# The expert layer of an encoder trunk: TensorE's wide products, transpositions of the middle columns and sums, kept in the order of the program

## The chip, the cores and the metric

The kernel runs on one core of one Trainium2 chip. The metric is the device time of one execution in microseconds (us); less is better. TensorE is called PE here (its weight loads PEld), VectorE DVE, ScalarE ACT, GpSimd POOL and SyncE SP. Each engine works off its own queue in order, and engines wait for each other by semaphores.

## The reference

It is a two-layer encoder over 272 tokens of 1024 columns: attention and a dense SwiGLU, then a two-way RWKV-7 scan and a mixture of experts, each with a layer norm behind it. The change touches the experts alone:

```python
logits = x @ w_router + b_router                    # 256 tokens that count, 8 experts
gates  = top-2 of softmax(logits), renormalized
for e in range(8):                                  # 1024 -> 3584 -> 1024
    y += gates[:, e:e+1] * ((silu(x @ w_gate[e]) * (x @ w_up[e])) @ w_down[e])
out = layer_norm(ALPHA * h + y)
```

All is float32. Each expert has 44 MB of weights, all of which are read once.

## The kernel before

**Passes.** By the tokens that chose them, five experts are made wide (W, up to 128 tokens) and three narrow (N, up to 64); they are worked off in the order W N W W N W W N. Each expert is worked off in two halves of 1792 middle columns, so the loop `for n in range(16)` in `moe` (lines 1585 to 1637) has 16 passes, 0 to 15; passes 2, 3, 8, 9, 14 and 15 are narrow. A pass computes gate and up products for its half (x is the stationary operand, the weights stream), and between and behind them the down products of the half of the pass before (`down`, `down_wide`, `down_narrow`).

**Wide products.** A product in float32 is made of three faster ones. Each piece of 768 to 1024 columns of weights (called a part here) is cast on ACT to `w_hi` (line 124), and the rest `w_lo` = raw - `w_hi` is made on DVE or, for three parts of twelve, on POOL (line 127). There are four buffers of `w_hi` and four of `w_lo`. `stream_wide` (line 1404) then issues, for each of 16 parts of gate or up, four products on `w_hi` and two on `w_lo` (line 1414). `down_wide` issues through `mm3` (lines 134 to 136) one on `w_hi`, one on `w_lo`, and one on `w_hi` with the rest of the activations. Narrow products take the raw weights in full float32 (lines 1429 and 1478); they need neither cast nor rest.

**Middle columns.** The activations `hid` are made by a Silu on ACT (lines 1616 and 1627) and a multiplication on DVE (lines 1621 and 1629), then transposed on PE (lines 1445 and 1459) through the one PSUM tile `pt` into `hth` (and `htl`), of which there is one buffer: `step` functions that are called in the stream of the next pass behind parts 2, 6, 10 and 14.

**Gathers and sums.** The tokens of the next expert are gathered by products with a one-hot matrix (lines 1359, 1366, 1385, 1393), also through `pt`. The finished expert is copied from PSUM (line 1498 or 139) and summed into the tokens by products (line 1512) and a multiply-add on DVE (line 1514).

**The order.** The text of the program doesn't set the order inside an engine's queue. A planner takes each instruction as soon as it believes, by its own estimates of all durations and of the landing of loads, that its operands and buffers are there; among several the earlier in the text goes first. `keep_in_program_order` binds an instruction behind the one traced just before it on the same engine. That is an order of issue only: it adds no semaphore and no wait for that one's end. Before the change it binds the narrow products (lines 1429 and 1478) and a few others. Weights are loaded by SP (line 1556) into a ring of 17 buffers of 0.9 MB, in the order of the program.

Of the kernel before, what the change touches and what calls it, by code (L numbers as in the profile page):

```python
# [26 lines left out]
FT = 1792  # L27
NB = FT // 128
# [66 lines left out]
class Trunk:  # L95
# [15 lines left out]
    def load(self, src, r0, kt, c0, nc_, pitch):  # L111

        raw = next(self.raws)()[:, :kt * nc_].rearrange("p (k c) -> p k c", k=kt)
        self.nc.sync.dma_start(raw, self.row_ap(src, r0 * pitch + c0, [[pitch, 128], [128 * pitch, kt], [1, nc_]]))
        return raw
# [13 lines left out]
            self.parted_pool = self.parted  # L129
        return hi, lo  # L130

    def mm3(self, ps, wh, wl, xh, xl, start, stop):
        mm = self.nc.tensor.matmul
        mm(ps, wh, xh, start=start, stop=False)  # L134
        mm(ps, wh, xl, start=False, stop=False)  # L135
        return mm(ps, wl, xh, start=False, stop=stop)  # L136

    def split(self, hi, lo, src, eng=None):
        return self.nc.scalar.copy(hi, src), (eng or self.nc.vector).tensor_tensor(lo, src, hi.bitcast(F32), op=OP.subtract)
# [1264 lines left out]
    def stream_wide(self, psum, xe, load, steps):  # L1404

        ps = [psum.tile([128, 2, 512], F32, name="pgu", bufs=2) for _ in range(2)]
        mm = self.nc.tensor.matmul
        for k in range(NF):
            raw = load(k)
            for a in range(2):  # L1410
                wh, wl = self.part_of(raw[:, 896 * a:896 * a + 896])
                for i, (x, w) in enumerate(((0, wh), (1, wh), (0, wl))):
                    for b in range(2):
                        mm(ps[a][:, b, :448], xe[:, x, k, :], w[:, 448 * b:448 * b + 448], start=k == 0 and i == 0,  # L1414
                           stop=k == NF - 1 and i == 2)
                for f in steps.pop(2 * k + a, ()):
                    f()
        return ps
# [16 lines left out]
    def hidden_wide(self, mp, psum, s, H):  # L1435

        nc = self.nc

        def step(i0):
            if i0 == 0:  # L1440
                H['h'] = [mp.tile([128, NB, 128], F32R, name=n, bufs=1) for n in ("hth", "htl")]
            n = min(4, NB - i0)
            pt = psum.tile([128, 4, 128], F32, name="pt", bufs=1)
            for j in range(n):
                nc.tensor.transpose(pt[:, j, :], s[:, i0 + j:FT:NB], self.ident)  # L1445
            hh, hl = H['h']
            self.split(hh[:, i0:i0 + n, :], hl[:, i0:i0 + n, :], pt[:, :n, :])

        return [lambda i=i: step(i) for i in range(0, NB, 4)]

    def hidden_narrow(self, mp, psum, s, H):
        nc = self.nc

        def step(i0):
            if i0 == 0:
                H['h'] = mp.tile([128, NB, 64], F32, name="hth", bufs=1)
            pt = psum.tile([128, 7, 64], F32, name="pt", bufs=1)
            for j in range(7):
                nc.tensor.transpose(pt[:, j, :], s[64:128, i0 + j:FT:NB], self.ident[64:128, 64:128])  # L1459
            nc.vector.tensor_copy(H['h'][:, i0:i0 + 7, :], pt)  # L1460

        return [lambda i=i: step(i) for i in (0, 7)]

    def down_wide(self, h, load, pd, half, first, last):
        hh, hl = h
        for j in range(4 * half, 4 * half + 4):
            raw, cut = load(j), (0, 1024, FT) if j % 2 == 0 else (0, 768, FT)
            for a, b in zip(cut, cut[1:]):
                wh, wl = self.part_of(raw[:, a:b])
                for o, n, i, q, c in self.pieces(j, a, b):  # L1470
                    self.mm3(pd[q][:, c:c + n], hh[:, i, :], hl[:, i, :], wh[:, o - a:o - a + n], wl[:, o - a:o - a + n],
                             first and i == 0, last and i == NB - 1)

    def down_narrow(self, h, load, pd, half, first, last):
        for j in range(4 * half, 4 * half + 4):
# [15 lines left out]
    def combine(self, mp, psum, n, G, pd, last=False):  # L1491

        nc, Y = self.nc, {}

        def parts(q):
            if len(pd) == 1:
                Y[0] = Y[1] = [mp.tile([128, 512], F32, name="xs", bufs=1)]
                nc.scalar.copy(Y[0][0], pd[0][0])
                return
            y = mp.tile([128, 2, NF, 128], F32R, name=G['tag'], bufs=1).rearrange("p i f t -> p i (f t)")  # L1500
            Y[q] = [y[:, i, 512 * q:512 * q + 512] for i in range(2)]
            self.split(*Y[q], pd[q][0])

        def add(q, t):
            if last:

                ps = psum.tile([128, 512], F32, name=f"pd{q}", bufs=1) if t == 0 else wide()[:, q, :]
            else:
                ps = psum.tile([128, 512], F32, name=pd[q % len(pd)][1], bufs=1)
            os = G['os'][q][:, t, :]  # L1510
            for i, x in enumerate(Y[q]):
                nc.tensor.matmul(ps, os, x, start=i == 0, stop=i == len(Y[q]) - 1)  # L1512
            y = self.ymoe[:, t, 512 * q:512 * q + 512]
            nc.vector.scalar_tensor_tensor(y, ps, self.gate[:, t, n:n + 1], y, op0=OP.mult, op1=OP.add)

        def wide():
            if 'w' not in Y:
                Y['w'] = psum.tile([128, 2, 512], F32, name="pgu", bufs=2)
            return Y['w']

        if last:
            return [lambda: parts(0)] + [lambda q=q, t=t: add(q, t) for t in range(2) for q in range(2)]
        if len(pd) == 1:
            return [lambda: parts(0)] + [lambda q=q, t=t: add(q, t) for q in range(2) for t in range(2)]
        return [f for q in range(2) for f in (lambda q=q: parts(q), lambda q=q: add(q, 0), lambda q=q: add(q, 1))]

    def moe(self, ep, psums, scanp):
# [221 lines left out]
```

## Time and profile before

| | us |
|---|---|
| median of 3 runs | 1858.39 (1857.37 to 1863.82) |
| the profiled execution | 1862.5 |
| its span, first to last instruction | 1860.4 |
| PE busy in the span | 1699.6 (91%) |
| DVE busy | 1276.6 (69%) |
| ACT busy | 913.0 (49%) |
| POOL busy | 631.1 (34%) |

The expert layer takes from about 890 us of the span to about 1845 us. A row of a timeline gives the start (us from the span's start), the length, the engine, the line, output<-inputs and a count, and in brackets how long the engine was idle before it and what ended that. Rows that run on overlap a little, since matmuls are pipelined: the pace is read from start to start. In the windows, PEclk is the share of PE's full clock (2.4 GHz) that was granted.

### The profile page before, as it was taken

Reading aid. Unit: us, or ns where it says so; the run is one execution under the profiler, and the core shown is the slowest. Engines: PE = TensorE matmul, PEld = TensorE weight load, DVE = VectorE, ACT = ScalarE, POOL = GpSimd, SP = SyncE. Lnnn points to the kernel's source line nnn. Section 1 sums busy time; section 2 is a strip of 40 time slices with the busy share of each in tenths; the row PEclk is TensorE's granted clock in tenths of the full one; section 3 lists DMA queues with packets and bytes.
Section 4 is the critical chain, followed back from the end, with each engine's and each line's share of the span. In section 5 each row is a group of like instructions: output and inputs, shape, how many; then the busy total and the mean of one; then the engine's idle time right before and its main releaser. Section 6 shows DMA issues by size and latency. Waiting matters only on the chain.

```text
span 1860.4 us, 30513 instructions
## 1 busy us (share of the span) xinstructions
PE 1699.6 (91%) x11422; PEld 1359.5 (73%) x11422; DVE 1276.6 (69%) x2135; ACT 913.0 (49%) x1612; POOL 631.1 (34%) x551
## 2 busy tenths in 40 slices
PE   6999899987988988897999999999999999999996
PEld 5888899975666766676986567888856668888552
DVE  5786655578868896854896446989934469899332
ACT  4575444446334435433674235766723357677210
POOL 4322300148464554512353112444502125445101
PEclk9999899988978878897999999999999999999998
DMA  6322455541101000355769899998999999899992
GB/s 203 120 91 69 136 182 177 186 125 47 57 24 53 24 25 2 131 204 215 241 238 348 347 426 426 425 342 305 341 358 352 423 422 345 327 328 345 389 395 92
DMA packets 130737, 431.79 MB, mean 232 GB/s; under 512 B 13689, under 2 KB 78674, under 8 KB 130578
## 3 DMA queue, kind: packets, MB, share of 16 engines
q1 hardware_dynamic: 127202, 427.78, 61.6%
q10 hardware_dynamic: 3376, 1.95, 0.4%
q8 instruction: 92, 1.51, 0.3%
q14 instruction: 67, 0.55, 0.1%
HBM read 428.66 MB, written 1.05 MB: 231 GB/s over the span
## 4 chain that ended last, share of the span: by engine, by line
PE 38%; issue 5%; DVE 4%; POOL 1%; DMA 1%; ACT 1%; SPq 0%; DVEq 0%; POOLq 0%; ACTq 0%
PE pgu L1414 16%; PE pgu L1429 5%; PE pdn L1478 4%; PE pd L135 3%; PE pd L136 3%; PE pd L134 3%; DVE w_lo L127 2%; POOL w_lo L127 1%; DMA w_raw<-in_moe_w_down_dram 1%; PE pd L1512 1%; DVE hid L1621 1%; PE pt L1445 1%; PE pt L1359 1%; PE pt L1459 1%; ACT w_hi L124 0%
## 5 line engine op out<-in xcount | busy, mean ns | idle before, releaser
L127 DVE TENSOR_TENSOR w_lo<-w_raw,w_hi 128x896 fp32r<-128x896 f32 (+2 forms) x445 | 647.2, 1494 | 151.5 <-ACT w_hi L124 144.5
L124 ACT CAST w_hi<-w_raw 128x896 fp32r<-128x896 f32 (+2 forms) x580 | 537.2, 960 | 279.5 <-PE pd L136 70.6
L127 POOL TENSOR_TENSOR w_lo<-w_raw,w_hi 128x1024 fp32r<-128x1024 f32 (+1 forms) x135 | 335.3, 2484 | 629.6 <-ACT w_hi L124 445.3
L1414 PE MATMUL pgu<-w_hi,xe 128*128 128x448 f32 x1280 | 299.5, 369 | 2.4 <-DVE hid L1621 1.6
L1414 PEld LDWEIGHTS pgu<-w_hi,xe 128*128 128x128 f32 x1280 | 237.5, 188 | 26.8 <-issue 6.5
L1414 PE MATMUL pgu<-w_lo,xe 128*128 128x448 f32 x640 | 164.6, 369 | 4.7 <-DVE w_lo L127 4.6
L1429 PE MATMUL pgu<-w_raw,xs 128*64 128x448 f32 x768 | 158.1, 544 | 0.0
L1414 PEld LDWEIGHTS pgu<-w_lo,xe 128*128 128x128 f32 x640 | 118.5, 188 | 18.9 <-DVE w_lo L127 8.1
L135 PE MATMUL pd<-w_lo,hth 128*128 128x512 f32 (+1 forms) x320 | 121.3, 384 | 9.8 <-DVE w_lo L127 6.3
L136 PE MATMUL pd<-w_hi,htl 128*128 128x512 f32 (+1 forms) x320 | 119.8, 375 | 0.0
L1429 PEld LDWEIGHTS pgu<-w_raw,xs 128*64 128x64 f32 x768 | 59.1, 136 | 81.1 <-issue 76.9
L134 PE MATMUL pd<-w_hi,hth 128*128 128x512 f32 (+1 forms) x320 | 101.0, 375 | 4.1 <-ACT w_hi L124 4.1
L135 PEld LDWEIGHTS pd<-w_lo,hth 128*128 128x128 f32 x320 | 62.1, 194 | 28.7 <-DVE w_lo L127 8.3
L1478 PE MATMUL pdn<-w_raw,hth 128*64 128x512 f32 (+1 forms) x384 | 79.6, 542 | 0.0
L134 PEld LDWEIGHTS pd<-w_hi,hth 128*128 128x128 f32 x320 | 58.9, 194 | 17.3 <-ACT w_hi L124 5.7
L134 PE MATMUL pj<-xh,w_hi 128*128 128x272 f32 x192 | 60.1, 313 | 11.8 <-ACT w_hi L124 5.4
L136 PEld LDWEIGHTS pd<-w_hi,htl 128*128 128x128 f32 x320 | 62.2, 194 | 10.3 <-issue 0.7
L1478 PEld LDWEIGHTS pdn<-w_raw,hth 128*64 128x64 f32 x384 | 32.5, 137 | 37.8 <-issue 30.4
L136 PE MATMUL pj<-xh,w_lo 128*128 128x272 f32 x192 | 58.3, 304 | 0.6 <-DVE w_lo L127 0.6
L135 PE MATMUL pj<-xl,w_hi 128*128 128x272 f32 x192 | 58.0, 302 | 0.0
L1629 DVE TENSOR_TENSOR hid<-hid,pgu 64x896 f32<-64x896 f32 x12 | 13.0, 1091 | 62.3 <-ACT hid L1627 62.3
L153 POOL COPY ln_s<-ln_y 128x272 f32<-128x272 f32 x2 | 0.8, 414 | 156.2 <-DVE ln_y L150 156.2
(639 smaller groups left out, 3569.6 us busy)
## 6 DMA issues: line engine op xcount, KB each, us to landing
w_raw<-in_moe_w_down_dram SPq DMA_DIRECT2D x128, 896.0 KB, 7.5
w_raw<-in_moe_w_gate_dram SPq DMA_DIRECT2D x126, 896.0 KB, 7.8
w_raw<-in_moe_w_up_dram SPq DMA_DIRECT2D x126, 896.0 KB, 7.2
w_raw<-in_attn_w_in_dram SPq DMA_DIRECT2D x12, 1024.0 KB, 9.0
w_raw<-in_rw_w_rkv_dram SPq DMA_DIRECT2D x12, 1024.0 KB, 5.3
w_raw<-in_ffn_w_gate_dram SPq DMA_DIRECT2D x11, 1024.0 KB, 7.3
w_raw<-in_ffn_w_up_dram SPq DMA_DIRECT2D x11, 1024.0 KB, 5.2
w_raw<-in_ffn_w_down_dram SPq DMA_DIRECT2D x8, 1024.0 KB, 5.0
```

Of the source, the lines that this page charges most:

```text
L124: nc.scalar.copy(hi, raw)
L127: self.parted = eng.tensor_tensor(lo, raw, hi.bitcast(F32), op=OP.subtract)
L134: mm(ps, wh, xh, start=start, stop=False)
L135: mm(ps, wh, xl, start=False, stop=False)
L136: return mm(ps, wl, xh, start=False, stop=stop)
L1359: nc.tensor.matmul(ps[:, j, :], self.h3[:, t, 128 * f:128 * f + 128], G['og'][:, t, :], start=t == 0, stop=t == 1)
L1414: mm(ps[a][:, b, :448], xe[:, x, k, :], w[:, 448 * b:448 * b + 448], start=k == 0 and i == 0, stop=k == NF - 1 and i == 2)
L1429: self.tc.keep_in_program_order(self.nc.tensor.matmul(ps[a][64 * h:64 * h + 64, b, :448], xs[:, k, :], raws[h][:, o:o + 448], start=k == 0 ...
L1445: nc.tensor.transpose(pt[:, j, :], s[:, i0 + j:FT:NB], self.ident)
L1459: nc.tensor.transpose(pt[:, j, :], s[64:128, i0 + j:FT:NB], self.ident[64:128, 64:128])
L1478: self.tc.keep_in_program_order(self.nc.tensor.matmul(pd[64 * q:64 * q + 64, c:c + n], h[:, i, :], raw[:, o:o + n], start=first and i == 0 ...
L1512: nc.tensor.matmul(ps, os, x, start=i == 0, stop=i == len(Y[q]) - 1)
```

## The change

`keep_in_program_order` is put around the wide products of gate and up, the three products of `mm3` where `down_wide` calls it, the transpositions of the middle columns (wide and narrow) and the sums. The gathers and all other callers of `mm3` stay as they were, as do all other engines' instructions and the loads. The block behind `tc.If(most > 0)`, for experts with more tokens than places, calls the same functions.

```diff
-    def mm3(self, ps, wh, wl, xh, xl, start, stop):
+    def mm3(self, ps, wh, wl, xh, xl, start, stop, keep=lambda i: i):
         mm = self.nc.tensor.matmul
-        mm(ps, wh, xh, start=start, stop=False)
-        mm(ps, wh, xl, start=False, stop=False)
-        return mm(ps, wl, xh, start=False, stop=stop)
+        keep(mm(ps, wh, xh, start=start, stop=False))
+        keep(mm(ps, wh, xl, start=False, stop=False))
+        return keep(mm(ps, wl, xh, start=False, stop=stop))
...
     def stream_wide(self, psum, xe, load, steps):
-        mm = self.nc.tensor.matmul
+        mm = lambda *a, **kw: self.tc.keep_in_program_order(self.nc.tensor.matmul(*a, **kw))
...
     def hidden_wide(self, mp, psum, s, H):
-                nc.tensor.transpose(pt[:, j, :], s[:, i0 + j:FT:NB], self.ident)
+                self.tc.keep_in_program_order(nc.tensor.transpose(pt[:, j, :], s[:, i0 + j:FT:NB], self.ident))
...
     def hidden_narrow(self, mp, psum, s, H):
-                nc.tensor.transpose(pt[:, j, :], s[64:128, i0 + j:FT:NB], self.ident[64:128, 64:128])
+                self.tc.keep_in_program_order(
+                    nc.tensor.transpose(pt[:, j, :], s[64:128, i0 + j:FT:NB], self.ident[64:128, 64:128]))
...
     def down_wide(self, h, load, pd, half, first, last):
                     self.mm3(pd[q][:, c:c + n], hh[:, i, :], hl[:, i, :], wh[:, o - a:o - a + n], wl[:, o - a:o - a + n],
-                             first and i == 0, last and i == NB - 1)
+                             first and i == 0, last and i == NB - 1, self.tc.keep_in_program_order)
...
     def combine(self, mp, psum, n, G, pd, last=False):
-                nc.tensor.matmul(ps, os, x, start=i == 0, stop=i == len(Y[q]) - 1)
+                self.tc.keep_in_program_order(nc.tensor.matmul(ps, os, x, start=i == 0, stop=i == len(Y[q]) - 1))
```

## Rows read from the trace of the kernel before

**Rows 1.** The page: busy time by engine; its row of the wide products on `w_hi`.

```profile
PE 1699.6 (91%) x11422; PEld 1359.5 (73%) x11422; DVE 1276.6 (69%) x2135; ACT 913.0 (49%) x1612; POOL 631.1 (34%) x551
L1414 PE MATMUL pgu<-w_hi,xe 128*128 128x448 f32 x1280 | 299.5, 369 | 2.4 <-DVE hid L1621 1.6
```

**Rows 2.** Windows: stretch, us; busy (count) PE, PEld, DVE, ACT, POOL; clock, DMA share, GB/s.

```profile
1002.80:1055.00 52.20, 52.20 (x276) 31.08 (x275) 24.60 (x23) 19.93 (x26) 9.48 (x4) 1.00 0.85 323
1360.00:1419.90 59.90, 56.61 (x276) 35.25 (x275) 24.14 (x23) 20.37 (x26) 9.79 (x4) 0.94 0.96 369
1095.00:1360.00 265.00, 256.39 (x1277) 216.33 (x1273) 223.61 (x171) 169.75 (x201) 108.60 (x45) 0.99 0.96 371
```

**Rows 3.** Waits of PE, 850 to 1861: who waited for whom, us, times, longest.

```profile
PE pd L135 <- DVE w_lo L127: 6.3, 5, 2.1
PE pt L1445 <- DVE hid L1621: 5.7, 6, 1.3
PE pgu L1414 <- DVE w_lo L127: 4.6, 6, 1.0
PE pd L135 <- POOL w_lo L127: 3.3, 5, 0.9
```

**Rows 4.** Timeline of PE in pass 5, second down half: start, length, [idle before].

```profile
1213.75 0.62 PE L134 MATMUL pd<-w_hi,hth 128*128 128x512 f32 x2
1215.68 0.73 PE L1445 MATMUL pt<-blob,hid 128*128 128x128 f32 x4 [1.31 <-DVE hid L1621]
```

**Rows 5.** Timelines of PE, DVE and POOL in the same pass.

```profile
1194.33 1.78 PE L1414 MATMUL pgu<-w_hi,xe 128*128 128x448 f32 x8
1196.76 1.78 PE L1414 MATMUL pgu<-w_hi,xe 128*128 128x448 f32 x8
...
1197.41 14.92 DVE L127 TENSOR_TENSOR w_lo<-w_raw,w_hi 128x896 fp32r<-128x896 f32 x9
1213.55 2.08 DVE L1621 TENSOR_TENSOR hid<-hid,pgu 128x896 f32<-128x896 f32 x2 [1.22 <-PE pgu L1414]
...
1211.84 2.76 POOL L127 TENSOR_TENSOR w_lo<-w_raw,w_hi 128x1024 fp32r<-128x1024 f32 x1 [2.47 <-ACT w_hi L124]
```

**Rows 6.** End of narrow pass 8: timelines of PE and ACT, then windows of the clock.

```profile
1395.36 0.72 PE L134 MATMUL pd<-w_hi,hth 128*128 128x512 f32 x2 [2.07 <-ACT w_hi L124]
1396.02 1.05 PE L1459 MATMUL pt<-blob,hid 64*128 64x64 f32 x7
1397.82 0.80 PE L135 MATMUL pd<-w_lo,hth 128*128 128x512 f32 x1 [0.76 <-POOL w_lo L127]
...
1391.83 0.91 ACT L1627 ACTIVATE hid<-pgu 64x896 f32<-64x896 f32 x1 [10.29 <-PE pgu L1429]
1394.26 3.46 ACT L124 CAST w_hi<-w_raw 128x1024 fp32r<-128x1024 f32 x4
...
1396.00:1400.00 4.00, 3.25 (x13) 2.68 (x13) 3.92 (x3) 1.74 (x4) 1.77 (x1) 0.61 1.00 421
1400.00:1404.00 4.00, 4.00 (x14) 3.38 (x14) 1.86 (x2) 2.08 (x3) 2.38 (x1) 0.54 1.02 430
```

**Rows 7.** Narrow pass 2: timeline of ACT, then of PE.

```profile
1007.06 1.78 ACT L124 CAST w_hi<-w_raw 128x1024 fp32r<-128x1024 f32 x2 [3.78 <-DMA w_raw<-in_moe_w_down_dram]
...
1015.62 0.50 PE L134 MATMUL pd<-w_hi,hth 128*128 128x512 f32 x1
```

**Rows 8.** Start of wide pass 5, behind a narrow expert: timelines of ACT and PE.

```profile
1156.15 0.59 ACT L1498 COPY xs<-pdn 128x512 f32<-128x512 f32 x1 [12.44 <-PE pdn L1478]
...
1156.79 1.12 PE L1512 MATMUL pdn<-xs,os_n 128*128 128x512 f32 x2 [0.68 <-ACT xs L1498]
1177.66 0.67 PE L1414 MATMUL pgu<-w_lo,xe 128*128 128x448 f32 x2 [0.98 <-DVE w_lo L127]
```

**Rows 9.** Timeline of PE in the last pass and behind it.

```profile
1812.71 1.02 PE L1459 MATMUL pt<-blob,hid 64*128 64x64 f32 x7 [0.83 <-DVE hid L1629]
1825.33 1.02 PE L1459 MATMUL pt<-blob,hid 64*128 64x64 f32 x7 [0.72 <-DVE hth L1460]
```

## The prediction, made before the change was run

> **What bounds the kernel now.** I read the page first, then the windows, the waits, and the timelines around each long wait. PE is busy in 91% of the span [rows 1], so the question is how much idle time of PE the expert layer holds, and behind what. The windows give the first half of it: in 1095 to 1360, four wide passes behind each other, PE is busy 256.4 of 265 us [rows 2], so 8.6 us are idle. DVE is busy 223.6 there and POOL 108.6. How close these two are to being the bound is seen in one stream [rows 5]: nine `w_lo` of DVE run in 14.92 us without a gap, and with three of POOL that is twelve parts, 4.97 us for four. PE needs 2.43 us for two parts (start 1194.33 to start 1196.76), 4.86 for four. PE is the bound by 2% at most, and lives off a lead of four buffers. The waits show the same: of PE's longest sorts of wait in the layer three are for `w_lo`, 6.3 + 4.6 + 3.3 = 14.2 us, and one, 5.7 us, for `hid` in front of transpositions [rows 3].
>
> The second place is the joint between a narrow and a wide pass. Pass 8 with the down products of pass 7 takes 59.9 us, pass 2 with those of pass 1 only 52.2 [rows 2], with the same 276 instructions of PE. In pass 8 ACT has the Silu (L1627) in its queue ahead of the casts of the down weights, waits 10.29 us for PE, and so the first cast starts when the narrow products are over; PE waits 2.07 and 0.76 us and then runs with a granted clock of 0.61 and 0.54 in 1396 to 1404 [rows 6]. In pass 2 ACT casts as soon as the weights land (1007.06), and PE has put down products between the narrow ones (1015.62) [rows 7].
>
> So the present order already lies near the text: the planner moves things by a few products, but for four kinds of place: a part's `w_hi` ahead of the `w_lo` of the part before; transpositions pulled ahead; sums pulled ahead; and pass 2. Going through the timelines of the 16 passes against the text, I find no other move of more than the gathers, which stay free.
>
> **The change part by part.** It adds no instruction, no wait and no load; nothing on SP's or POOL's queue is bound. What counts is what PE may no longer do while it waits, since its queue is in order: behind a product that waits for `w_lo` stands the rest of the layer. The block for overflowing experts doesn't run: 1280 products on `w_hi` [rows 1] are 5 wide experts x 2 halves x 2 streams x 16 parts x 4.
>
> (a) Transpositions of wide passes. In the second down half of a wide pass the transpositions of its own `hid` are pulled ahead and wait 1.31 us for DVE's two multiplications (PE free at about 1214.2, next start 1215.68) [rows 4, 5]. Such waits of 1.3 us are in passes 5, 7, 11 and 13; six in all are 5.7 us [rows 3]. Bound behind part 2 of the next pass they come some 13 us later, when `hid` is long there. What is late next is the rest of the first down part: POOL ends it at 1211.84 + 2.76 = 1214.60, so PE goes on at about 1214.7 instead of 1216.2, behind the transpositions; these are still to be done later and hold PE some 0.4 us (of their 0.73 the end overlaps the next), so 1.1 remain. 4 x 1.1 = 4.4 saved; bounds 0 (DVE, which has three more parts behind the multiplications, holds PE up anyway) and 5.7.
>
> (b) Narrow transpositions. In the last pass they are pulled ahead of the down products and wait 0.83 us; behind these, the second set waits 0.72 for the copy of the first [rows 9]. Afterwards the first wait is gone and the second stays, since `hth` has one buffer: 0.8 saved (0 to 0.83). In passes 8 and 14 such a set (1.05 us) now fills part of the wait for the first `w_lo` of the down products, between 1396.02 and 1397.82 [rows 6]. Without the filler the wait is as long and the set comes later: 2 x 0.95 = 1.9 lost (0 to 1.9).
>
> (c) Sums. Pass 5 starts behind a narrow expert. ACT's queue has the copy of its sums first, idle for 12.44 us, and PE waits 0.68 for it [rows 8]; then sums and transpositions fill the time until the first parts are cast. Bound behind parts 3, 5, 7 and 9 they fill nothing: the first `w_hi` is there about 0.7 + 1.0 us after the copy begins, so PE waits some 1.9 instead of 0.7 us, then about 1.3 for the rest by POOL, and still owes two sums (1.12 each [rows 8], 0.8 without overlap) and two sets of transpositions (0.5 each): 2.6. That is up to 2.5 us late, but at the pass's twelfth part PE waits 0.98 for DVE anyway [rows 8], whose work hasn't grown, and there most of it is swallowed. I take 0.5 for each of passes 5 and 11: 1.0 lost (0 to 5).
>
> (d) Wide products. Now PE issues eight products on `w_hi` (two parts), then four on `w_lo` [rows 5]; afterwards four and two. The first rest of a pair is wanted 0.81 us earlier. Where PE waits for DVE now it has usually only one later block behind it, two products on `w_hi` of the down part (0.47 us). The waits end when DVE ends, so what is lost is just that which PE did ahead: 0.47 at three joints, 1.4 us. No row shows a strict stream, so the bounds are wide: 0, and that all waits for `w_lo` double, 14.2 [rows 3].
>
> (e) Pass 2. Its narrow products run first, then 16 down parts. If ACT's casts of the first four stay ahead of the Silu, where they are now [rows 7], PE finds four parts ready and only the fifth, made on POOL (2.76) behind a cast of 1 us, is tight: 1.0 lost. Bounds: 1 us won (fewer changes between the two kinds of product), and 59.9 - 52.2 = 7.7 lost, if it comes to look like pass 8.
>
> The sum: -4.4 - 0.8 + 1.9 + 1.0 + 1.4 + 1.0 = +0.1 us on the profiled execution's 1862.5 (span 1860.4 and 2.1 around it). That execution is 4.1 us above the median of the runs, within their spread; carried over to the median, 1858.39 + 0.1 = 1858.5.
>
> On (c) a rule of the Trainium skill speaks against the change. By "TensorE: Matmul & The Clock Gate", section "HAM oscillation — how this bites in real kernels", an engine that idles waiting for its operand is set back to half its clock, and the products behind the wait are paid double. The trace agrees in pass 8 (0.61 and 0.54). By that rule both restarts of (c) would cost (0.39 + 0.46) x 4 = 3.4 us more each, and the sum would be +6.9.
>
> **The rivals.** *Slower, by the restart.* The mechanism: at a joint nothing is cast when PE arrives, and PE, bound to the order, idles until it falls to 1.2 GHz. Places: the down products in pass 2 (7.7 lost instead of 1.0) and the starts of passes 5 and 11 (2.5 + 3.4 each instead of 0.5). 0.1 + 6.7 + 10.8 = +17.6, 1876. It decides where ACT's queue puts the copy or the Silu ahead of the casts and nothing else is bound earlier. For it: ACT has that order in rows 6 and 8. Against it: in pass 2 it hasn't [rows 7]. With pass 2 alone it is +6.8, 1865.
>
> *Slower, by the rests.* Each wait for `w_lo` doubles: +14.2 in place of 1.4, 1871. For it: 4.97 against 4.86 us [rows 5], no lead is regained in a stream. Against it: DVE's work isn't more, and a rest of the first part of a pair gives its buffer back 0.81 us earlier, too. The skill's "SBUF — State Buffer", section "Who interferes with whom", says that DVE, when it reads two operands from SBUF, and GpSimd lock each other out, which speaks for this rival: the rows agree, since 14.92 us hold nine parts of DVE and three of POOL without gain from running side by side.
>
> *Faster.* With PE bound, the planner places ACT's and DVE's work anew. If the casts of the down weights go ahead of the Silu in passes 8 and 14 as they do in pass 2, each wins up to 7.7: 1858.5 - 15.4 = 1843. For it: ACT stands idle 10.29 us there [rows 6]. Against it: nothing of the change touches ACT, and the Silu is earlier in the text.
>
> *It doesn't do what it says.* As the order is nearly that of the text, little moves: within 2 us of 1858.
>
> **How the numbers follow.** Forecast 0.46, its own range 1851 to 1867; restart 0.15, rests 0.13, faster 0.14, no effect 0.12. A measurement of this kernel tells apart 0.5%, 9.3 us: below 1849.1 or above 1867.7. Faster: 0.14 + 0.08 from the forecast's lower tail = 0.22. Slower: 0.13 + 0.11 of the restart (its weaker form is within) + 0.05 = 0.29. Within: 0.49. The range leaves out a tenth at either side: it ends inside the faster case, 1845, and short of the restart's full price, 1873.
>
> **What would show it.** (a): no wait for `hid` in front of L1445. (b): the 0.83 gone; L1459 behind the down products in pass 8. (c): PE's first idle time in pass 5 above 0.68, no sum before part 3. (d): four products on `w_hi`, then two on `w_lo`, and about the same 14 us of waits. (e): 16 narrow parts in one piece in pass 2, with ACT's casts at their start. The prediction fails if the clock drops at a joint where it was full, or if ACT's queue has the casts and the Silu in another order than now.

## The result: 0.64% slower, 1875.4 us

The changed kernel takes 1875.38 us (median of 12 runs, 1865.17 to 1882.32), the kernel before on the same chip 1863.36 (12 runs); the ratio is 1.0064 with a 95% interval of 1.0040 to 1.0087, some 12 us. Predicted were 1858.5 us and, as likeliest, no difference. Of the 16.9 us between forecast and result, 5.0 are the kernel before: the forecast stood on the median of three runs, 1858.39, and twelve give 1863.36.

Two spans of the trace are used below. The *layer* runs from the start of the first wide product to the start of the last down product: 947.8 us before (890.2 to 1838.0 us of the span), 956.0 after (895.6 to 1851.6), +8.3. The 22.4 us behind it are the same in both, and the first wide product starts between 886 and 900 us in the profiles of the sixteen kernels, in no relation to the edits. So +8.3 us are the change's, within the interval of the ratio (7 to 16 us), and the rest isn't shown to be.

The page after: busy time by engine, and its rows of the rests by DVE and POOL and of the wide products on `w_hi` [rows 1].

```profile
PE 1710.0 (91%) x11422; PEld 1361.1 (73%) x11422; DVE 1263.3 (67%) x2135; ACT 925.0 (49%) x1612; POOL 633.6 (34%) x551
L127 DVE TENSOR_TENSOR w_lo<-w_raw,w_hi 128x896 fp32r<-128x896 f32 (+2 forms) x445 | 639.5, 1470 | 180.5 <-ACT w_hi L124 179.3
L127 POOL TENSOR_TENSOR w_lo<-w_raw,w_hi 128x1024 fp32r<-128x1024 f32 (+1 forms) x135 | 337.9, 2504 | 643.2 <-ACT w_hi L124 572.5
L1407 PE MATMUL pgu<-w_hi,xe 128*128 128x448 f32 x1280 | 321.1, 373 | 6.4 <-ACT w_hi L124 3.7
```

PE's waits after, from 850 us on (who waited for whom: us, times, longest), to be laid beside [rows 3]:

```profile
PE pd L135 <- DVE w_lo L127: 12.7, 7, 2.3
PE pd L135 <- POOL w_lo L127: 6.1, 9, 1.9
...
PE pgu L1407 <- DVE w_lo L127: 4.3, 7, 1.0
PE pgu L1407 <- ACT w_hi L124: 3.7, 3, 1.5
...
PE pgu L1407 <- POOL w_lo L127: 2.2, 2, 1.1
```

The 5.7 us of waits for `hid` in front of L1445 are gone, and the waits for `w_lo` have grown from 14.2 to 12.7 + 6.1 + 4.3 + 2.2 = 25.3 us. 8.3 of these are for parts that POOL makes, and all 17.0 for DVE's stand behind a part that lay beside one of POOL's (start and end of both in the trace; before, 10.2 of 10.9). All waits of PE in the layer went from 32.5 to 37.0 us (the sum of the bracketed idle times). Most of the rest of the difference between these two traces goes with the clock. Windows after, columns as in [rows 2]: pass 2, pass 8, and four stretches behind waits:

```profile
1010.90:1063.40 52.50, 52.47 (x273) 30.40 (x272) 24.61 (x22) 20.79 (x26) 9.58 (x4) 1.00 0.95 380
1372.30:1431.30 59.00, 56.26 (x275) 32.20 (x274) 24.56 (x23) 20.89 (x26) 9.74 (x4) 0.97 0.98 371
...
1004.00:1007.00 3.00, 3.00 (x10) 2.34 (x9) 1.07 (x3) 1.04 (x1) 0.00 (x0) 0.58 0.89 294
1300.00:1303.50 3.50, 3.50 (x10) 2.68 (x10) 1.70 (x2) 1.70 (x2) 0.00 (x0) 0.51 0.92 356
...
1536.00:1540.00 4.00, 3.53 (x9) 3.14 (x10) 4.00 (x3) 2.48 (x3) 2.69 (x2) 0.50 1.01 425
1600.50:1603.50 3.00, 3.00 (x8) 2.30 (x7) 1.88 (x2) 1.04 (x1) 0.00 (x0) 0.50 0.96 315
```

PE is busy in nearly all of the last four stretches and gets half its clock. Taking 4 us windows over the whole layer, and 4 x (1 - clock) of each below 0.97, the time so lost is 8.4 us before and 12.0 after. So +4.5 us of waits and +3.5 of half clock make the 8.3 but for 0.3. That these two are a full account isn't shown: for the wide down products alone, below, the same sum gives 4.3 of 9.3 us. Nor is the clock's part shown to be the change's. Over the 12 runs of the changed kernel the mean granted clock of the whole execution goes from 0.939 to 0.946, and the one profiled has 0.939, where the kernel before was profiled at 0.945.

What a wait looks like: timelines of the changed kernel in the second down half of pass 11 (POOL, DVE, PE).

```profile
1595.95 2.38 POOL L127 TENSOR_TENSOR w_lo<-w_raw,w_hi 128x1024 fp32r<-128x1024 f32 x1 [2.70 <-ACT w_hi L124]
...
1596.86 2.56 DVE L127 TENSOR_TENSOR w_lo<-w_raw,w_hi 128x1024 fp32r<-128x1024 f32 x1
...
1597.03 0.40 PE L134 MATMUL pd<-w_hi,hth 128*128 128x512 f32 x1
1599.47 0.50 PE L135 MATMUL pd<-w_lo,hth 128*128 128x512 f32 x1 [2.05 <-DVE w_lo L127]
```

POOL starts a part at 1595.95; the part that DVE begins 0.9 us later lasts 2.56 us, ends 1.1 us behind POOL's, and it is the one that PE wants next. Waits of 2.04 to 2.05 us for a part beside POOL's stand in passes 1, 5 and 6 as well, and one of 2.34 in pass 12. The clock drops behind those in passes 1, 6 and 11. Behind the other two it stays at 1.00; their rows of PE and a window behind each:

```profile
1229.83 0.50 PE L135 MATMUL pd<-w_lo,hth 128*128 128x512 f32 x1 [2.04 <-DVE w_lo L127]
1669.87 0.50 PE L135 MATMUL pd<-w_lo,hth 128*128 128x512 f32 x1 [2.34 <-DVE w_lo L127]
...
1230.00:1234.00 4.00, 4.00 (x21) 3.38 (x22) 2.74 (x3) 2.25 (x3) 0.25 (x1) 1.00 0.82 266
1670.00:1674.00 4.00, 4.00 (x21) 3.39 (x22) 2.78 (x3) 2.20 (x3) 0.20 (x1) 1.00 0.77 262
```

### The profile page after: what moved, and what is told of

It reads as the page before. It is cut to its first block, busy times and chain, and to the rows that moved or that the text cites. A ratio compares the mean times of both kernels' runs of the same rounds, so it can differ in the third digit from the quotient of the medians.

```text
span 1874.0 us, 30406 instructions
## 1 busy us (share of the span) xinstructions
PE 1710.0 (91%) x11422; PEld 1361.1 (73%) x11422; DVE 1263.3 (67%) x2135; ACT 925.0 (49%) x1612; POOL 633.6 (34%) x551
## 3 DMA queue, kind: packets, MB, share of 16 engines
q8 instruction: 92, 1.51, 0.3%
## 5 line engine op out<-in xcount | busy, mean ns | idle before, releaser
L127 DVE TENSOR_TENSOR w_lo<-w_raw,w_hi 128x896 fp32r<-128x896 f32 (+2 forms) x445 | 639.5, 1470 | 180.5 <-ACT w_hi L124 179.3
L124 ACT CAST w_hi<-w_raw 128x896 fp32r<-128x896 f32 (+2 forms) x580 | 547.5, 960 | 275.7 <-PE pgu L1407 81.6
L1407 PE MATMUL pgu<-w_hi,xe 128*128 128x448 f32 x1280 | 321.1, 373 | 6.4 <-ACT w_hi L124 3.7
L1407 PE MATMUL pgu<-w_lo,xe 128*128 128x448 f32 x640 | 184.5, 371 | 6.8 <-DVE w_lo L127 4.3
L135 PE MATMUL pd<-w_lo,hth 128*128 128x512 f32 (+1 forms) x320 | 124.4, 389 | 19.7 <-DVE w_lo L127 12.7
L134 PE MATMUL pd<-w_hi,hth 128*128 128x512 f32 (+1 forms) x320 | 120.0, 375 | 1.6 <-ACT w_hi L124 1.6
L1429 PEld LDWEIGHTS pgu<-w_raw,xs 128*64 128x64 f32 x768 | 52.2, 136 | 80.4 <-issue 78.0
L135 PEld LDWEIGHTS pd<-w_lo,hth 128*128 128x128 f32 x320 | 61.7, 193 | 42.1 <-DVE w_lo L127 17.3
L139 DVE TENSOR_TENSOR htl<-pt,hth 128x512 fp32r<-128x512 f32 (+1 forms) x40 | 24.6, 615 | 59.3 <-ACT hth L139 59.3
L139 ACT CAST hth<-pt 128x512 fp32r<-128x512 f32 (+1 forms) x40 | 21.3, 533 | 75.7 <-PE pt L1445 75.7
L135 PE MATMUL pj<-xl,w_hi 128*128 128x272 f32 x192 | 57.5, 300 | 0.0
```

The lines of the kernel that those rows point to most:

```text
L124: nc.scalar.copy(hi, raw)
L127: self.parted = eng.tensor_tensor(lo, raw, hi.bitcast(F32), op=OP.subtract)
L134: keep(mm(ps, wh, xh, start=start, stop=False))
L135: keep(mm(ps, wh, xl, start=False, stop=False))
L1407: mm = lambda *a, **kw: self.tc.keep_in_program_order(self.nc.tensor.matmul(*a, **kw))
L1429: self.tc.keep_in_program_order(self.nc.tensor.matmul(ps[a][64 * h:64 * h + 64, b, :448], xs[:, k, :], raws[h][:, o:o + 448], start=k == 0 ...
```

## The experiments

Three theories: **R**, the order itself costs, since PE has nothing to do ahead; **F**, the free transpositions and sums were fillers; **Q**, later sharpened into **P**, the new order shifts which part of DVE lies beside one of POOL. In the first four expectations the time is counted to the end of the span (970.2 and 978.4), 22.4 us more than the layer. Where a pass is said to be longer or shorter, it runs from the last down product of the pass before to its own last one.

### One edit alone: transpositions

The changed kernel without the edits to wide products, `mm3` and sums:

```diff
-        mm = lambda *a, **kw: self.tc.keep_in_program_order(self.nc.tensor.matmul(*a, **kw))
+        mm = self.nc.tensor.matmul
...
-                             first and i == 0, last and i == NB - 1, self.tc.keep_in_program_order)
+                             first and i == 0, last and i == NB - 1)
...
-                self.tc.keep_in_program_order(nc.tensor.matmul(ps, os, x, start=i == 0, stop=i == len(Y[q]) - 1))
+                nc.tensor.matmul(ps, os, x, start=i == 0, stop=i == len(Y[q]) - 1)
```

> Of the four edits only the transpositions of the middle columns (wide and narrow) are bound to the text; products and sums are free. From the first wide product to the end of the span the kernel before takes 970.2 us, the changed one 978.4. Theory R (rests: the loss comes from PE having nothing to do ahead while it waits for w_lo in the bound products): the waits for hid go and nothing is lost, 4 to 6 us shorter than before (965 us; ratio 0.997). Theory F (fillers: DVE is late in the second down halves whatever PE does, so the transpositions cost nothing there and cost their full time, 0.9 to 1.1 us each set, later): six wide passes by 1 to 1.5 us, 6 to 9 us longer (977 us; ratio 1.004). Theory Q (queues: only all edits together make the planner place DVE's multiplications between the w_lo): within 2 us of before.

Measured: layer 949.4 us (+1.7), ratio 1.0014 (1.0003 to 1.0024). R and F are both off. Passes 3, 4, 9, 10, 15 and the end, at or behind a narrow half, are 3.3 us shorter, but passes 5, 7, 11 and 13, where waits for `hid` should have been saved, are 5.6 us *longer*. The same place in pass 7 in both kernels shows why. Before (DVE, POOL, ACT, PE):

```profile
1347.90 2.08 DVE L1621 TENSOR_TENSOR hid<-hid,pgu 128x896 f32<-128x896 f32 x2 [1.33 <-PE pgu L1414]
1351.64 1.22 DVE L127 TENSOR_TENSOR w_lo<-w_raw,w_hi 128x1024 fp32r<-128x1024 f32 x1
...
1352.91 2.40 POOL L127 TENSOR_TENSOR w_lo<-w_raw,w_hi 128x1024 fp32r<-128x1024 f32 x1 [4.07 <-ACT w_hi L124]
...
1351.78 1.85 ACT L124 CAST w_hi<-w_raw 128x1024 fp32r<-128x1024 f32 x2 [3.23 <-PE pd L136]
...
1350.04 0.73 PE L1445 MATMUL pt<-blob,hid 128*128 128x128 f32 x4 [1.31 <-DVE hid L1621]
```

With the transpositions alone bound (in DVE's second row two parts, 0.87 us and 3.42):

```profile
1348.13 2.08 DVE L1622 TENSOR_TENSOR hid<-hid,pgu 128x896 f32<-128x896 f32 x2 [1.38 <-PE pgu L1414]
1351.00 4.29 DVE L127 TENSOR_TENSOR w_lo<-w_raw,w_hi 128x768 fp32r<-128x768 f32 x2
...
1351.48 2.72 POOL L127 TENSOR_TENSOR w_lo<-w_raw,w_hi 128x1024 fp32r<-128x1024 f32 x1 [2.47 <-ACT w_hi L124]
...
1350.36 1.05 ACT L124 CAST w_hi<-w_raw 128x1024 fp32r<-128x1024 f32 x1 [1.58 <-PE pd L136]
...
1351.14 0.50 PE L135 MATMUL pd<-w_lo,hth 128*128 128x512 f32 x1 [0.51 <-DVE w_lo L127]
1355.34 0.50 PE L135 MATMUL pd<-w_lo,hth 128*128 128x512 f32 x1 [1.71 <-DVE w_lo L127]
```

The third part of DVE behind the multiplications begins 3.74 us after they did, in both. Before, PE idled for `hid` and gave a buffer back late, ACT's cast waited 3.23 us for it, and POOL began only 5.01 us after them (1352.91): that part took 1.22 us. Now ACT waits 1.58 us, POOL begins after 3.35 us (1351.48), the part takes 3.42, and PE waits 1.71 us for it in place of the 1.31 saved.

### One edit alone: sums

As above, with only the line of the sums bound.

> Of the four edits only the sums of an expert's output are bound to the text. Prediction's term (c), which theories R and Q keep: 1 us longer, 0 to 5, all of it at the starts of passes 5 and 11 (971 us from the first wide product to the end; ratio 1.001). Theory F: the sums are fillers too, 20 of them in pairs at the starts of the passes behind a finished expert; each pass 0.5 to 1 us longer, 3 to 5 us in all (974 us; ratio 1.002).

Measured: layer 949.5 (+1.8), ratio 1.0015 (0.9997 to 1.0032): the size that term (c) and R gave, by the trace not F's (the runs' interval, -0.6 to 6 us, leaves F's 3 to 5 open). The place is another than (c)'s: passes 7, 11 and 13 are 2.0 to 2.1 us longer each, in 7 and 13 with two waits of 0.43 us for a `w_lo` of DVE in the gate stream, pass 12 is 1.5 us longer, and the passes at or behind a narrow half are 4.0 us shorter.

### One edit alone: wide products

Only the line `mm = lambda ...` of `stream_wide` is kept of the change.

> Of the four edits only the products of the wide streams are bound to the text, four on w_hi and two on w_lo for each part. Theory R: half of the waits for w_lo come from here, 3 to 5 us longer (974 us from the first wide product to the end; ratio 1.002). Theory F: PE is never short of products inside a stream, 0 to 1 us longer (971 us; ratio 1.000). Theory Q: within 2 us, with DVE's multiplications one behind the other as before.

Measured: layer 947.2 (-0.6), ratio 0.9985 (0.9968 to 1.0001). R is off: inside the streams the bound order costs nothing. Q's reason is off too: here, as in the changed kernel, a part stands between DVE's two multiplications in eight of the ten wide passes (before, in two), and no time is lost by it.

### One edit alone: wide down products

Only `mm3` with `keep_in_program_order` is kept of the change.

> Of the four edits only the wide down products are bound to the text. Theory R: most of the loss is here, the waits for w_lo in front of L135 go from 9.6 to 19 us and the time from the first wide product to the end by 7 to 9 us (978 us; ratio 1.004). Theory F: the free transpositions still fill the waits, 1 to 3 us longer (972 us; ratio 1.001). Theory Q: within 2 us, with DVE's multiplications one behind the other as before.

Measured: layer 957.0 (+9.3), ratio 1.0041 (1.0025 to 1.0056). R has the size, but not the place: waits in front of L135 go only from 9.6 to 11.3 us. The loss is 0.2 to 0.8 us in each of ten down halves of passes 1, 5, 7, 11 and 13 (4.9 in all), 3.9 us in passes 8 and 9, and 3.2 us in the second down half of pass 12; the other passes give 2.7 back. The 3.2 us go with the clock. Before, and with the down products bound, PE in that half:

```profile
1653.88 0.38 PE L135 MATMUL pd<-w_lo,hth 128*128 128x256 f32 x1 [2.10 <-DVE w_lo L127]
```

```profile
1670.02 0.58 PE L135 MATMUL pd<-w_lo,hth 128*128 128x256 f32 x1 [2.31 <-DVE w_lo L127]
```

and windows behind it, before and then here:

```profile
1654.00:1660.00 6.00, 6.00 (x30) 5.00 (x31) 4.23 (x5) 3.78 (x4) 1.25 (x1) 1.00 0.68 256
```

```profile
1670.00:1676.00 6.00, 5.98 (x15) 4.83 (x16) 3.16 (x4) 1.88 (x2) 0.00 (x0) 0.50 0.69 245
```

15 products where there were 30, but it isn't the 0.2 us that the wait is longer: behind one of 2.34 us at this place the changed kernel keeps its clock at 1.00, and so does this one in pass 6, behind one of 2.31, where the kernel before falls to half behind 2.07. Over the layer the half clock costs this kernel 8.5 us, as much as the one before. The four edits alone add up to 1.7 + 1.8 - 0.6 + 9.3 = +12.2 us, together they make +8.3.

### No part on POOL, in both kernels

```diff
-            self.on_pool = (0, 4, 8)
+            self.on_pool = ()
```

The changed kernel with it:

> The changed kernel with every w_lo of the expert layer on DVE, none on POOL. Measured so far from the first wide product to the last down product's start: 947.8 us before, 956.0 changed, and 949.4, 949.5, 947.2, 957.0 with only the transpositions, sums, wide products, wide down products bound. In the traces a w_lo of DVE takes 1.07 us where POOL makes none and 1.9 to 2.1 us where POOL makes one beside it (2.5 us). Theory P (collisions: PE waits where a w_lo of DVE that it needs next lies beside one of POOL; which one that is has been shifted by the new order): without POOL four parts take DVE 4.3 us against 4.97, less than PE's 4.86; nearly all waits for w_lo (25 us) go, 20 to 25 us shorter than the changed kernel: 933 us, ratio to before 0.990. Theory R (order: PE has nothing to do ahead): the waits get shorter but the bound order still loses 5 to 8 us against the free one with the same parts. Rival: DVE gets 119 parts more, 127 us of work, and is the bound: 5 to 20 us longer than the changed kernel.

Measured: layer 913.5 us (-42.5 to the changed kernel), 1828.69 us, ratio to before 0.9829 (0.9807 to 0.9850). The page's row of the rests and PE's two longest waits for operands in the layer:

```profile
L127 DVE TENSOR_TENSOR w_lo<-w_raw,w_hi 128x896 fp32r<-128x896 f32 (+2 forms) x563 | 613.1, 1120 | 141.5 <-ACT w_hi L124 124.4
```

```profile
PE pd L135 <- DVE w_lo L127: 5.2, 9, 0.9
...
PE pgu L1407 <- ACT w_hi L124: 3.6, 3, 1.5
```

DVE makes 118 parts more than in the changed kernel and is busy 26 us *less* with them (613.1 to 639.5). The gain is nearly twice what P gave. The kernel before with it:

> The kernel before with every w_lo of the expert layer on DVE, none on POOL. Theory P: its waits for w_lo (14 us) go, 933 to 936 us from the first wide product to the last down product's start, within 3 us of the changed kernel without POOL; ratio 0.992. Theory R: 5 to 8 us shorter than the changed kernel without POOL. Rival (DVE the bound): 5 to 20 us longer than the kernel before.

Measured: layer 928.6, ratio 0.9901 (0.9873 to 0.9928). P has the direction; but the changed kernel is now 15.1 us shorter than this one, where P expected the two alike and R the changed one longer. R falls here. Of the 15.1 us, 12.1 stand in the narrow passes 8, 9 and 14, and P has no reason for them.

### The same parts, another place

```diff
-            self.on_pool = (0, 4, 8)
+            self.on_pool = (1, 5, 9)
```

> The changed kernel with the same number of parts on POOL, each one part later (parts 1, 5, 9 of twelve in place of 0, 4, 8). Theory P: another w_lo of DVE lies beside POOL's, so the waits in the second down halves change: at least 3 us longer or shorter than the changed kernel (956.0), pass by pass in the same places (the wait of 2.1 us in front of L135 goes or moves). Theory R: the order of PE is the same, so within 2 us of the changed kernel.

Measured: layer 925.7 us, ratio 0.9880 (0.9854 to 0.9906): -30.4 us with PE's bound products in the same order, but for one pair of parts, and as many parts on POOL. It isn't quite as much work: 40 of POOL's 119 parts, those of the down weights, have 768 columns here in place of 1024, 9% of its columns. By the 42.5 us that all of them are worth, 9% is an estimated 4 us, so most of the 30.4 is the place; place and columns were not run apart. The kernel before with it:

> The kernel before with POOL's parts each one later (1, 5, 9 of twelve). The changed kernel went from 956.0 to 925.7 us by that alone. Theory P (collisions set the sign of the change): the kernel before moves otherwise than the changed one did, so that the change's worth with POOL there is another than +8.3 us: 930 to 942 us, the change then worth -4 to -16. Theory R (the order itself costs 8): 917 to 919 us, so that the changed one is again 8 us longer.

Measured: 933.2, ratio 0.9927 (0.9903 to 0.9951). With (2, 6, 10), which gives POOL the same columns as (1, 5, 9), the kernel before:

> The kernel before with POOL's parts two later (2, 6, 10 of twelve). Theory P: 930 to 948 us, another difference to the changed kernel with the same parts than +8.3 us. Theory R: the changed one with the same parts is 7 to 9 us longer.

Measured: 943.8, ratio 0.9993 (0.9975 to 1.0011). And the changed one:

> The changed kernel with POOL's parts two later (2, 6, 10 of twelve). Theory P: the parts of the second down halves that lie beside POOL are others again: 920 to 950 us, at least 3 us from 956.0, and the change's worth with POOL there differs from +8.3 us by over 3 us. Theory R: 7 to 9 us longer than the kernel before with the same parts.

Measured: 920.8, ratio 0.9859 (0.9831 to 0.9887). P holds in all three.

### All edits but the wide down products

> The changed kernel with the wide down products free; wide products, transpositions and sums bound. Theory R (the loss is that of the bound down products, alone 9.3 us in the trace): 946 to 948 us, as before; ratio 0.999. Theory P: the other three edits shift the collisions too, and a good part stays: 950 to 955 us; ratio 1.004.

Measured: layer 952.7, ratio 1.0033 (1.0015 to 1.0051): P's, not R's.

### POOL subtracts beside DVE, and nobody waits for it

On top of the changed kernel without parts on POOL:

```diff
+        if self.again and self.n_parts % 12 in (0, 4, 8):
+            kept = self.again.tile([128, 384], F32, name="again", bufs=1)
+            nc.gpsimd.tensor_tensor(kept, raw[:, 0, :384], hi.bitcast(F32)[:, 0, :384], op=OP.subtract)
```

> The changed kernel with every w_lo on DVE, and POOL takes the first 384 columns of parts 0, 4 and 8 of twelve once more into a tile that nothing reads: PE waits for nothing that POOL makes. In the traces so far a part of POOL's ends 2.06 us after the part of DVE that ran at its start, and the part of DVE that began beside it ends 0.92 us after POOL's. Theory L (lock: one of the two stands while the other subtracts): 384 of 896 columns hold DVE up 0.86 us, four parts take 4.3 + 0.86 = 5.2 us against PE's 4.86, and up to 0.3 us in each of 119 fours come back as waits for w_lo of DVE: 930 to 950 us from the first wide product to the last down product's start (913.5 without). Theory T (POOL's parts cost because they come late to PE, not because DVE stands): 913 to 916 us, the waits for w_lo unchanged at 5 us.

Measured: layer 931.3 us, +17.8; ratio to before 0.9905 (0.9878 to 0.9933). The page's row of the rests and PE's longest wait in the layer:

```profile
L128 DVE TENSOR_TENSOR w_lo<-w_raw,w_hi 128x896 fp32r<-128x896 f32 (+2 forms) x563 | 685.3, 1267 | 105.9 <-ACT w_hi L125 104.0
```

```profile
PE pd L139 <- DVE w_lo L128: 10.9, 18, 1.7
```

DVE's same 563 parts take 72 us more. Theory L holds, T doesn't: what POOL costs is not only that its parts come late.

### POOL out of the second down halves alone

```diff
                 f, pd = (self.down_wide, pd) if KINDS[p] == 'W' else (self.down_narrow, pd[0])
+                self.on_pool = () if half else (0, 4, 8)
                 f(h, lambda j: load(2, expert[p], tl, j), pd, half, tl == 0, tl == 1)
+                self.on_pool = (0, 4, 8)
```

> The changed kernel with all parts of each second down half on DVE, POOL's places elsewhere as they are. Theory P in its narrow form (the loss arises where POOL's second part of a second down half holds up the part of DVE that PE needs next): the waits of 2.05 us in passes 1, 6 and 11 go, passes 5, 7, 11 and 13, 10.8 us longer than before, come to within 3 us of it, and the layer to 938 to 946 us (956.0). Wide form (collisions all over the layer, the streams of the gate products too): 948 to 954 us, with these four passes still over 5 us longer than before.

Measured: layer 939.3 us, ratio 0.9975 (0.9954 to 0.9996). The waits of 2.04 to 2.34 us are gone; passes 5, 7, 11 and 13 are still 3.7 us longer than before (in their gate streams), a little over the narrow form's 3. The kernel before with it:

> The kernel before with all parts of each second down half on DVE. Narrow form: it has fewer of these collisions than the changed one, so it wins less, 940 to 946 us (947.8), and the changed kernel is then not longer than this one by over 2 us. Wide form: 940 to 947 us, the changed kernel still 5 us or more longer.

Measured: layer 939.5, ratio 0.9960 (0.9939 to 0.9980). The difference between the two kernels is -0.2: in the layer of these two traces the narrow form holds for the sum. By the runs the changed one is 0.15% longer, some 3 us, with intervals that overlap. All pairs, layer in us (one trace each), and the quotient of the two ratios to the kernel before:

```
POOL's parts of twelve          before   changed   difference   by the runs
0, 4, 8                          947.8     956.0      +8.3        +0.64%
0, 4, 8, no second down half     939.5     939.3      -0.2        +0.15%
1, 5, 9                          933.2     925.7      -7.6        -0.47%
2, 6, 10                         943.8     920.8     -22.9        -1.34%
none                             928.6     913.5     -15.1        -0.73%
```

The changed kernel without parts on POOL beats both kernels, by 1.7% the one before.

## Why the prediction was wrong

**The step that failed is (a)**, and in it the sentence that POOL ends its part "at 1211.84 + 2.76 = 1214.60, so PE goes on at about 1214.7". It moved PE and left POOL and DVE where they stood. When PE stops idling for `hid`, it frees buffers earlier, ACT casts earlier, POOL starts earlier and stops DVE in the part that PE wants next. Forecast for passes 5, 7, 11 and 13: -4.4 us; measured +5.6 with the transpositions alone. With all edits it is +10.8, more than the whole loss, but not by (a) alone: the sums alone make the same four passes 5.6 us longer, and 10.0 of the 10.8 stand in their gate streams, through which sums and transpositions are now led. The bound 0 ("DVE ... holds PE up anyway") was on the wrong side.

**(d) was mis-sized.** Forecast +1.4, "0.47 at three joints". The streams gave -0.6 alone; the down products, where the 0.47 came from, +9.3 alone, most of it a little in each of ten down halves and in passes 8 and 9. The ends of the range, 0 and 14.2, held the true growth of the waits for `w_lo`, 11.1 us. That is the rival "by the rests", which had 0.13: most of its price of 14.2 came in, and so did its reason that DVE and POOL lock each other out; that the streams regain no lead did not cost anything by itself. The prediction's "PE is the bound by 2% at most" reads 4.97 against 4.86 the wrong way round: DVE with POOL is the slower. Rows 5 had it in plain sight: 14.92 us for nine parts of DVE [rows 5], 1.66 each, where a part alone takes 1.07. I read this as a load that stays the same, not as collisions whose places move.

**(b)** forecast +1.1 (-0.8 and +1.9). The wait of 0.83 [rows 9] is gone and the 0.72 stays, as written; the fillers in passes 8 and 14 cost nothing to lose. In the trace of the changed kernel, the second set behind the last pass, and the two waits in pass 8:

```profile
1838.93 1.02 PE L1460 MATMUL pt<-blob,hid 64*128 64x64 f32 x7 [0.72 <-DVE hth L1461]
...
1407.43 0.49 PE L134 MATMUL pd<-w_hi,hth 128*128 128x512 f32 x1 [0.81 <-ACT w_hi L124]
1409.85 0.80 PE L135 MATMUL pd<-w_lo,hth 128*128 128x512 f32 x1 [1.93 <-POOL w_lo L127]
```

0.81 + 1.93 in place of 2.07 + 0.76 [rows 6]: without the filler PE waits no longer than with it, so nothing was lost. Alone, the transpositions made these two passes 1.3 us shorter and the other passes at or behind a narrow half 3.3.

**(c)** was right on how pass 11 begins: no sum before part 3, four products and then two, and

```profile
1534.29 1.07 PE L1407 MATMUL pgu<-w_hi,xe 128*128 128x448 f32 x4 [1.51 <-ACT w_hi L124]
1536.47 1.12 PE L1407 MATMUL pgu<-w_lo,xe 128*128 128x448 f32 x2 [1.11 <-POOL w_lo L127]
```

1.51 and 1.11 us where 1.9 and 1.3 were forecast. Behind them the clock is 0.50 (1536 to 1540), as the rival "by the restart" had it and as the prediction named for a sign that it fails. Pass 5 begins with waits as long, 1.51 and 1.11, and keeps its clock at 1.00 (1166 to 1170). The gate stream of pass 11 is 3.3 us longer than before, that of pass 5 [rows 8] 1.9. The rival's other place, pass 2, didn't come to look like pass 8. (c)'s price was in its range, 1.8 us for the sums alone, by luck: it put nothing on passes 7 and 13, which got 2.0 us longer each, and nothing on those at or behind a narrow half, which got 4.0 shorter.

**(e)** was right but for its size: one piece of narrow products, then the down parts, 52.5 us in place of 52.2 [rows 2]; forecast +1.0.

**The faster rival** didn't come: pass 8 takes 59.0 us after 59.9 [rows 2].

## What to carry to other kernels

Before an instruction is moved, look for the engines that lock each other out near it: their pieces move along with every buffer that is freed sooner, so a wait taken away is priced only when the next two or three collisions have been redrawn. Where the sign of a change turns with a thing that it doesn't touch (here POOL's places), tune that thing first. An engine that helps should be priced by what it takes from its neighbour: compare the neighbour's busy time for more parts alone with that for fewer beside the helper.

## What the runs showed of the hardware

DVE and POOL don't subtract side by side. In the changed kernel, the part of DVE that runs when POOL begins ends first; POOL's part ends 2.06 us after that (mean of 66; in six more POOL began in the last 0.06 us of DVE's part), and the part that DVE begins meanwhile ends 0.92 us after POOL's (116 cases). A part of DVE takes 1.07 us where POOL makes none (176 parts) and 1.97 beside it (181). So a part on POOL takes an estimated 1.4 us of DVE's time (181 parts longer by 0.90, for 119 on POOL) to save 1.07. The Trainium skill's "SBUF — State Buffer", section "Who interferes with whom", says that DVE with two operands from SBUF contends with a GpSimd instruction that reads SBUF; these runs agree, and show the part of DVE standing until POOL's has ended. Its "GPSIMD Engine Reference", section "3.1 Elementwise — side-by-side cycle accounting", gives GpSimd about twice DVE's time for such an operation (1.96); here it is 2.13 us, for two parts of 896 columns on POOL with none of DVE beside them, to 1.08.

PE's granted clock isn't settled by the length of the wait before it. In the changed kernel it fell to half behind waits of 2.04, 2.05 and 2.05 us and stayed at 1.00 behind others of 2.04 and 2.34; two waits of 1.51 and 1.11 us were followed by 0.50 in pass 11 and by 1.00 in pass 5. What decides was not tried.
